# Attention in pieces of four heads, keys built by halves, and the output norm's mean subtracted from kept partial sums in DRAM by adding DMAs

## The chip, the cores and the metric

The kernel runs on one core of a Trainium2 chip. The metric is the device time of one execution in microseconds (us). Three runs before the change gave 1446.03, 1446.87 and 1447.19 us; the median is 1446.87. A profile is one more execution, taken with the hardware profiler.

Engines are named as in the profile: PE is TensorE (matrix products), with PEld for its weight loads, DVE is VectorE, ACT is ScalarE, POOL is GpSimd, SP is SyncE. DMAs are issued by SP (queue q1), by GpSimd (queue q0), and a few by ScalarE (q10). They all run on the core's 16 DMA engines. Only GpSimd's queue carries adding DMAs, which add the source to what the destination holds.

## The reference, cut to what matters

One layer over 1024 tokens and 2048 channels, all in float32:

```python
h = x @ w_in + b_in
q, k, v, g_attn, u_pool, g_pool = split(h)
a = banded_sink_attention(q, k, v, sinks, bias, valid) * silu(g_attn)
b = multiscale_pool(u_pool, w_pool, pool_scale) * silu(g_pool)
mix = concat([a, b]) @ w_out
ple = sigmoid(x @ w_gate_ple) * (p @ w_ple)
out = layer_norm(alpha * x + mix + ple, ln_gain, ln_bias)   # over the 2048 channels
```

Attention has 16 query heads of 64 and two key/value heads, each for eight query heads. A block of 128 queries sees its own and the previous block of keys; a learned sink joins each softmax. The norm first subtracts each token's mean over the channels.

## The kernel before, in words

**Layout and products.** Activations are kept as blocks of 128 channels by tokens, so the 2048 output channels are 16 blocks (`NB`), and the 1024 tokens come as two halves of `T` = 512. A float32 product is made from three fp32r products: each operand is split into a rounded high part and a low rest, and `mm3` (L182 to L185) issues high by high, low by high, high by low. ScalarE casts the high part (`wh`, L815), VectorE makes the low part (`wl`, L126). Large products use a Winograd scheme with seven products per pair of blocks (`p1` to `p7`); a pair is a `Job`, and the last two jobs of a stage, as the first two, run side by side.

**Stages.** `s1` and `s2` make keys, values and queries and the first half of everything else; `s3` finishes gates, pooling and the embedding; `s4` and `s5` are the two halves of the output product; `s6` is its rest. `s4` leaves 16 partial sums `co` in DRAM, 1024 tokens wide. `s5` adds the other half of the product for the first `F1` = 768 tokens in the Winograd scheme (384 columns to a matmul), `s6` does the last `F2` = 256 tokens plainly. In `s5` a job's result is finished by an adding DMA on GpSimd's queue, `part += co` (L436, `finished`); six steps later the result is squared for the norm (`norm_square`, L1022). The four blocks of the last two jobs go the other way: their `co` is loaded ahead into `filled` tiles, and products are added to it. In `s6` the rest of each `co` is loaded, and products are added.

**The mean.** The weights of the second half (`wc`) are centred in advance, so only the partial sums `co` carry a mean. While `s4` runs, `csum` adds up all 16 `co`; `mean_to_subtract` (early in `s5`) sums it over the 128 partitions by a product with ones and scales it by -1/2048 (L997). For blocks 4 to 7 `first_done` adds it on VectorE. For the other blocks `less_mean` (L1012) adds it by one more matmul per PSUM bank: operands `z` are the high and low part of the mean, stacked on 64 partitions each.

**Steps.** The program is written as a sequence of steps. One step is one product of a job (12 matmuls) and whatever is due then: `self.after(n, fn)` runs `fn` n steps on, `self.later(n, fn)` does so and holds its instructions behind the marked ones of that time. The tile framework then orders the instructions of each engine by this sequence among those that are ready, and sets the waits. Each engine runs its instructions in the order that results, and stops at one that has to wait. GpSimd's DMAs use eight semaphores in turn, so one waits until the eighth before it has landed.

**Units ahead.** A weight unit (a pair `wh`, `wl`) is made four products ahead (`take`), in a pool of four.

**Attention.** `heads(h, j)` handles two heads (block `j` of the queries) over one half `h` of the tokens: four query blocks `bq`. It runs beside `s2`, one call every nine steps. Scores (L607) are four matmuls of 256 keys, VectorE adds the bias and takes the maximum (L609), ScalarE takes exponentials (L623) and shares (L636), TensorE transposes (L643), and `value` (L663) multiplies by values (`vv`) and by the differences of neighbouring value blocks (`vd`), which take back what a window leaves out (`affine_select`, L651). Keys and values of the second key/value head are built after the eighth call: `k_build` for both halves in one go at step t+71, `v_build` by halves.

**The start.** `ple_inputs` loads the first embedding weights in two pieces with the first piece of `p` between; `ple_half` (L873) starts with products that need high parts only.

Of the kernel before, what the change touches and what calls it, by code (L numbers as in the profile page):

```python
# [31 lines left out]
P = 128  # L32
# [24 lines left out]
class Job:  # L57


    def __init__(self, w, b0, b1, half, first, done, tokens=2 * T, plain=False, ahead=None):  # L60
        self.ahead, self.filled, self.mean, self.apart, self.wait = ahead, False, False, False, 4
        self.w, self.b, self.half, self.first, self.done = w, (b0, b1), half, first, done
        self.tokens, self.plain = tokens, plain


class Layer:
# [396 lines left out]
    def product(self, job, o, s):  # L463
# [8 lines left out]
        mean = {"p1": 0, "p5": n}.get(o) if job.mean else None  # L472
        with self.in_turn("PE"):
            for k in range(4):
                f = slice(k * P, (k + 1) * P)
                mm = self.mm3(ps, (wh[:, f], wl[:, f]), (xh[:, k], xl[:, k]), k == 0 and o in s, k == 3 and mean is None)
# [22 lines left out]
    def run_plain(self, g):  # L499
# [3 lines left out]
        for i in range(2):  # L503
            ps = self.bank(BANKS[0][i], 2)[:, :F2]
            final = job.mean and i
            for u in range(2):
                wh, wl = self.take()
                for k in range(4):
                    f = slice(k * P, (k + 1) * P)
                    mm = self.mm3(ps, (wh[:, f], wl[:, f]), self.x_plain(4 * u + k), u + k == 0, False)  # L510
# [3 lines left out]
                if u:  # L514
                    mm = self.less_mean(ps, F1)
# [12 lines left out]
    def k_build(self, g, src):  # L528
# [5 lines left out]
        for h in range(2):  # L534
# [40 lines left out]
    def heads(self, h, j):  # L575
# [3 lines left out]
        rq, qs, sc, pt, old, pv, pre, bias = [], [], {}, {}, {}, {}, [], []  # L579

        def begin():
            rq.append(self.fetch(self.qd[j][:, h * T : h * T + T]))
            bias.append(self.slot()[:, :T].rearrange("p (e k) -> p e k", e=2))
            self.load(bias[0], self.rel[j])
# [10 lines left out]
        def k0(bq):  # L595
            return P if h == 0 and bq == 0 else 0

        def score(bq):
            sc[bq] = self.slot()[:, :T].rearrange("p (e k) -> p e k", e=2)
            ps = self.bank("sc", 2, (P, 2, 256))  # L600
            z = k0(bq)

            keys = slice((4 * h + bq - 1) * P + z, (4 * h + bq + 1) * P)
            for e in range(2):
                q = qs[e][:, bq * P : (bq + 1) * P]
                for i, kk in enumerate(self.kk):
                    nc.tensor.matmul(ps[:, e, z:], q, kk[:, keys], start=i == 0, stop=i == 1)  # L607
            for e in range(2):
                nc.vector.tensor_tensor_reduce(  # L609
                    out=sc[bq][:, e, z:], in0=ps[:, e, z:], in1=bias[0][:, e, z:], op0=ALU.add, op1=ALU.max, scale=1.0,  # L610
                    scalar=self.c(C_SINK + 8 * j + 2 * bq + e), accum_out=mx[:, 2 * bq + e : 2 * bq + e + 1])

        def shift(bq):
            f = slice(2 * bq, 2 * bq + 4)
            nc.vector.tensor_scalar(out=neg[:, f], in0=mx[:, f], scalar1=-1.0, scalar2=None, op0=ALU.mult)
            self.tt(sk[:, f], self.c(C_SINK + 8 * j + 2 * bq, 4), neg[:, f], ALU.add)
            nc.scalar.activation(sk[:, f], sk[:, f], AF.Exp)

        def softmax(bq):
            z, h2 = k0(bq), slice(2 * bq, 2 * bq + 2)  # L620
            for e in range(2):
                i = 2 * bq + e
                nc.scalar.activation(sc[bq][:, e, z:], sc[bq][:, e, z:], AF.Exp, bias=neg[:, i : i + 1],  # L623
                                     accum_out=den[:, i : i + 1])
            self.tt(den[:, h2], den[:, h2], sk[:, h2], ALU.add)
            nc.vector.reciprocal(out=rec[:, h2], in_=den[:, h2])

            cur = sc[bq][:, :, P:]
            if z == 0:
                self.tt(cur, sc[bq][:, :, 0:P], cur, ALU.add, nc.gpsimd)  # L630

        def share(bq):
            cur = sc[bq][:, :, P:]
            for e in range(2):
                i = 2 * bq + e
                nc.scalar.activation(cur[:, e], cur[:, e], AF.Copy, scale=rec[:, i : i + 1])  # L636

        def trans(bq):
            ps = self.bank("tr", 1)
            for i in range(2):  # L640
                for e in range(2):
                    o = (2 * i + e) * P
                    nc.tensor.transpose(ps[:, o : o + P], sc[bq + i][:, e, P:], self.ident)  # L643
            for i in range(2):
                t = ps[:, 2 * i * P : 2 * i * P + 2 * P].rearrange("p (e q) -> p e q", e=2)
                both = pt[bq + i] = self.slot(F32R)[:, :T].rearrange("p (s e q) -> p s e q", s=2, e=2)
                nc.scalar.copy(out=both[:, 0], in_=t)
                self.lo(both[:, 1], t, both[:, 0])
                if not k0(bq + i):
                    a = old[bq + i] = self.slot(F32R)[:, :T]  # L650
                    nc.gpsimd.affine_select(out=a.rearrange("p (c q) -> p c q", c=4), in_=both.rearrange("p s e q -> p (s e) q").bitcast(F32), pattern=[[0, 4], [-1, P]],  # L651
                                            compare_op=ALU.is_ge, fill=0.0, base=-1, channel_multiplier=1)

        def value(bq):
            if bq % 2 == 0:
                pv[0] = self.bank("pv", 1, (P, 2, 2, P))
            ps = pv[0]
            ms = [(self.vv[h][:, bq], pt[bq].rearrange("p s e q -> p (s e q)"))]
            if not k0(bq):
# [874 lines left out]
```

## Time and profile before

| | |
|---|---|
| median of three runs | 1446.87 us |
| the profiled execution, its span | 1447.21 us, 1445.5 us |
| first matmul of `s5`, of `s6`, and last of `s6` (start) | 1260.7, 1382.0, 1432.0 us |
| granted TensorE clock over the span | 0.997 |

A page gives busy time by engine, the span in 40 slices, the DMA queues, the chain of work that ended last and the costliest groups. Other views of the same trace group instructions by line and shape, list who waited for whom, show the instructions in order of time, and sum busy times or DMA traffic over a chosen stretch. Start times count from the start of the span. A matmul's duration overlaps that of the next one, so what a matmul takes of TensorE is the distance between two starts.

### The profile page before, as it was taken

The numbers are of one execution on the slowest core, as the hardware profiler recorded it, in microseconds if no ns is written. First come the engines' busy times: TensorE is split into PE (matmuls) and PEld (weight loads), VectorE is DVE, ScalarE is ACT, GpSimd is POOL, SyncE is SP. The second block draws the span as 40 slices with busy tenths as digits, with TensorE's granted clock in tenths as the row PEclk, the third lists the DMA queues.
The fourth block names the chain that finished last, engine by engine and source line by source line (L and its number), as shares of the span: only waits on it lengthen the run. The fifth ranks groups of instructions, "written<-read, shape, count | busy, mean of one in ns | idle before, by whom it ended". The sixth has DMA issues, their size and how long they took to land.

```text
span 1445.5 us, 20558 instructions
## 1 busy us (share of the span) xinstructions
PE 1429.9 (99%) x6940; PEld 1216.4 (84%) x6940; DVE 1118.4 (77%) x2078; ACT 795.8 (55%) x1598; POOL 233.4 (16%) x339
## 2 busy tenths in 40 slices
PE   9999999999999999999999999999999999999996
PEld 7888888888888888888888888888888888899996
DVE  6859578888788888888768876867678666987787
ACT  6646376665666666566664444442456433654476
POOL 0000202122122111112101211111001211111223
PEclk9999999999999999999999999999999999999998
DMA  9463886454455454556887879998699768594476
GB/s 357 181 241 119 228 221 193 164 178 161 146 183 211 166 178 162 183 208 205 225 248 208 229 205 285 338 277 269 197 297 314 210 184 229 136 280 113 114 236 234
DMA packets 112457, 307.67 MB, mean 213 GB/s; under 512 B 12832, under 2 KB 18592, under 8 KB 112352
## 3 DMA queue, kind: packets, MB, share of 16 engines
q1 hardware_dynamic: 87712, 225.88, 45.6%
q0 software_dynamic: 21312, 73.15, 21.4%
q10 hardware_dynamic: 3328, 7.34, 1.5%
q8 instruction: 54, 0.88, 0.3%
q14 instruction: 51, 0.42, 0.1%
HBM read 207.75 MB, written 98.57 MB: 212 GB/s over the span
## 4 chain that ended last, share of the span: by engine, by line
PE 95%; DVE 2%; DMA 1%; ACT 1%; issue 0%; POOL 0%; SPq 0%; POOLq 0%; DVEq 0%; ACTq 0%
PE qa L183 16%; PE qa L184 16%; PE qa L185 16%; PE qb L184 12%; PE qb L183 12%; PE qb L185 12%; PE sc L607 2%; PE pv L663 2%; PE sc L185 1%; PE sc L183 1%; PE sc L184 1%; PE tr L643 1%; DMA cw<-in_wout 1%; PE tr L873 1%; PE pv L873 1%
## 5 line engine op out<-in xcount | busy, mean ns | idle before, releaser
L815 ACT CAST wh<-raw 128x512 fp32r<-128x512 f32 x428 | 264.1, 619 | 371.6 <-PE qa L184 142.6
L126 DVE TENSOR_TENSOR wl<-raw,wh 128x512 fp32r<-128x512 f32 x428 | 297.1, 698 | 106.6 <-ACT wh L815 101.9
L423 ACT COPY part<-qa 128x512 f32<-128x512 f32 (+1 forms) x180 | 103.9, 577 | 81.8 <-PE qa L185 79.3
L126 DVE TENSOR_TENSOR part<-part,qb 128x512 f32<-128x512 f32 (+1 forms) x120 | 81.3, 677 | 45.5 <-PE qb L185 38.8
L183 PE MATMUL qa<-b11h,wh 128*128 128x512 f32 (+2 forms) x292 | 109.2, 374 | 0.4 <-ACT part L423 0.4
L183 PE MATMUL qb<-b21h,wh 128*128 128x512 f32 (+2 forms) x292 | 109.1, 374 | 0.0
L185 PE MATMUL qa<-b11h,wl 128*128 128x512 f32 (+2 forms) x292 | 108.9, 373 | 0.0
L184 PE MATMUL qa<-b11l,wh 128*128 128x512 f32 (+2 forms) x292 | 108.9, 373 | 0.0
L185 PE MATMUL qb<-b21h,wl 128*128 128x512 f32 (+2 forms) x292 | 108.8, 372 | 0.0
L184 PE MATMUL qb<-b21l,wh 128*128 128x512 f32 (+2 forms) x292 | 108.7, 372 | 0.0
L183 PE MATMUL qa<-t4h,wh 128*128 128x512 f32 (+1 forms) x260 | 100.0, 385 | 0.5 <-DVE part L126 0.5
L183 PE MATMUL qa<-t2h,wh 128*128 128x512 f32 (+1 forms) x260 | 100.3, 386 | 0.1
L183 PE MATMUL qb<-t1h,wh 128*128 128x512 f32 (+1 forms) x260 | 100.2, 385 | 0.0
L183 PE MATMUL qb<-b22h,wh 128*128 128x512 f32 (+1 forms) x260 | 100.1, 385 | 0.0
L183 PE MATMUL qa<-t3h,wh 128*128 128x512 f32 (+1 forms) x260 | 100.1, 385 | 0.0
L185 PE MATMUL qa<-t2h,wl 128*128 128x512 f32 (+1 forms) x260 | 99.9, 384 | 0.0
L185 PE MATMUL qb<-t1h,wl 128*128 128x512 f32 (+1 forms) x260 | 99.8, 384 | 0.0
L185 PE MATMUL qb<-b22h,wl 128*128 128x512 f32 (+1 forms) x260 | 99.8, 384 | 0.0
L185 PE MATMUL qa<-t3h,wl 128*128 128x512 f32 (+1 forms) x260 | 99.8, 384 | 0.0
L184 PE MATMUL qa<-t2l,wh 128*128 128x512 f32 (+1 forms) x260 | 99.8, 384 | 0.0
L184 PE MATMUL qb<-b22l,wh 128*128 128x512 f32 (+1 forms) x260 | 99.8, 384 | 0.0
L184 PE MATMUL qa<-t3l,wh 128*128 128x512 f32 (+1 forms) x260 | 99.8, 384 | 0.0
(336 smaller groups left out, 3537.8 us busy)
## 6 DMA issues: line engine op xcount, KB each, us to landing
raw<-in_win SPq DMA_DIRECT2D x65, 512.0 KB, 4.2
h<-part SPq DMA_DIRECT2D x34, 512.0 KB, 2.9
part<-h POOLq DMA_DIRECT2D x34, 512.0 KB, 6.6
cw<-in_wout SPq DMA_DIRECT2D x64, 256.0 KB, 3.1
raw<-in_wgate SPq DMA_DIRECT2D x32, 512.0 KB, 4.4
raw<-wc SPq DMA_DIRECT2D x32, 512.0 KB, 4.3
s<-in_x SPq DMA_DIRECT2D x44, 256.0 KB, 6.6
wc<-cw SPq DMA_DIRECT2D x32, 256.0 KB, 2.4
```

Of the source, the lines that this page charges most:

```text
L126: return (eng or self.nc.vector).tensor_tensor(out=out, in0=a, in1=b, op=op)
L183: mm(ps, wh, xh, start=start, stop=False, skip_group_check=True)
L184: mm(ps, wh, xl, start=False, stop=False, skip_group_check=True)
L185: return mm(ps, wl, xh, start=False, stop=stop, skip_group_check=True)
L423: self.mark("ACT", self.nc.scalar.copy(out=dst, in_=ps))
L607: nc.tensor.matmul(ps[:, e, z:], q, kk[:, keys], start=i == 0, stop=i == 1)
L643: nc.tensor.transpose(ps[:, o : o + P], sc[bq + i][:, e, P:], self.ident)
L663: nc.tensor.matmul(ps[:, bq % 2], w, t, start=i == 0, stop=i == len(ms) - 1)
L815: ins = self.nc.scalar.copy(out=out, in_=a)
L873: mm = self.nc.tensor.matmul(ps[b], w[u][:, b, k], p[v], start=k == 0 and u + v == 0, stop=k == 1 and at in ((3, 5) if n == 0 else (4, 5)) ...
```

## The change

Five things change.

- **The mean.** `less_mean` is no longer a matmul. When the total is scaled, 28 adding DMAs on GpSimd's queue add it to `co` in DRAM: 12 of 128x768 (all blocks but 4 to 7) and 16 of 128x256. The 12 + 16 matmuls and the preparation of `z` go. The loads of the `filled` blocks, which now have to follow, move from step 20 to 26 of `s5`, those of the last operand from 30 to 34.
- **Attention.** A call of `heads` handles two query blocks of four heads (`j` and `j + 1`) over half of a token half. Each `value` matmul has 512 columns instead of 256. Scores come two to a step. Queries, bias and results are moved by two DMAs each per call instead of one.
- **Keys** of the second head are built by halves, at steps t+65 and t+77.
- **The start.** The first embedding weights are loaded and split in one piece, and `ple_half` uses `mm3` block by block.
- Two steps that split the operands of `s4` move from 26 and 30 to 28 and 31.

```diff
@@ product / run_plain
-        mean = {"p1": 0, "p5": n}.get(o) if job.mean else None
...
-        if mean is not None:
-            mm = self.less_mean(ps, mean)
...
-                if u:
-                    mm = self.less_mean(ps, F1)
@@ k_build
-        for h in range(2):
+        for h in src:
@@ heads
-    def heads(self, h, j):
+    def heads(self, h, j, half):
...
+            for i in range(2):
+                self.load(two(q)[:, i], self.qd[j + i][:, f])
+            for i in range(2):
+                bias.append(self.slot()[:, :T].rearrange("p (e k) -> p e k", e=2))
+                self.load(bias[i], self.rel[j + i])
...
+        def value(n):
+            ps = self.bank("pv", 1)
+            ms = [(self.vv[h][:, block(n)], t) for t in pt[n]]
+            if not none(n):
+                ms += [(self.vd[h][:, block(n) - 1 + h], t) for t in old[n]]
             for i, (w, t) in enumerate(ms):
-                nc.tensor.matmul(ps[:, bq % 2], w, t, start=i == 0, stop=i == len(ms) - 1)
+                nc.tensor.matmul(ps, w, t, start=i == 0, stop=i == len(ms) - 1)
...
-        for bq in range(4):
-            t = 4 * (bq // 2)
-            self.after(5 + 2 * bq, lambda bq=bq: score(bq))
...
+        for n in range(2):
+            for i in range(2):
+                self.after(6 + 4 * n, lambda n=n, i=i: score(n, i))
+            self.after(9 + 4 * n, lambda n=n: shift(n))
+            self.after(15 + 4 * n, lambda n=n: trans(n))
...
+            self.after(21 + 4 * n, lambda n=n: value(n))
@@ ple_inputs / ple_half
-        self.load(first[:, 0, : T // 2], w[:, 0, : T // 2])
+        self.load(first[:, 0], w[:, 0])
...
-                for at, (b, u, v) in enumerate(((0, 0, 0), (0, 1, 0), (1, 0, 0), (0, 0, 1), (1, 0, 1), (1, 1, 0)) if n == 0 else
...
+                for b in range(2):
+                    mm = self.mm3(ps[b], tuple(t[:, b, k] for t in w), tuple(t[:, 2 * h + k] for t in self.ple_p), k == 0, k == 1)
@@ mean_to_subtract / less_mean
-        step = self.one["new"]("q")[:, :h]
...
-    def less_mean(self, ps, k):
-        return self.nc.tensor.matmul(ps, self.w64, self.z[k], start=False, stop=True, skip_group_check=True)
+    def less_mean(self, b, f):
+
+        self.nc.gpsimd.dma_start(out=self.co[b][:, f], in_=self.total[:, f], accum_op=ALU.add)
@@ run
-            self.after(t - 2 + 9 * i, lambda i=i: self.heads(i % 2, i // 2))
-        self.after(t + 63 + 8, lambda: build_kv(KB, self.k_build, 1))
+            self.after(t - 2 + 9 * i, lambda i=i: self.heads(i // 2 % 2, i // 4 * 2, i % 2))
+        for h, n in enumerate((65, 77)):
+            self.after(t + n, lambda h=h: build_kv(KB, self.k_build, 1, (h,)))
...
-                    self.after((10, 13, 16, 19, 22, 26, 30)[n], step)
+                    self.after((10, 13, 16, 19, 22, 28, 31)[n], step)
...
-            self.after(20 + 2 * b, lambda b=b: self.load(flat(filled[b]), co[b][:, :F1]))
+            self.after(26 + 2 * b, lambda b=b: self.load(flat(filled[b]), co[b][:, :F1]))
...
+        for n, b in enumerate((8, 9, 0, 1, 2, 3, *range(10, NB))):
+            self.after(12 + n, lambda b=b: self.less_mean(b, slice(0, F1)))
+        for b in range(NB):
+            self.after(24 + b, lambda b=b: self.less_mean(b, slice(F1, 2 * T)))
```

What this does to the order on three engines. First GpSimd, early in `s5`, before: `co_212` to `co_227` are the partial sums of blocks 0 to 15, `d` and `part` the results to which L436 adds them.

```order
L145 DMA co_227<-part_11883 128x1024
L436 DMA d_12243<-co_216 128x768
L436 DMA d_12245<-co_218 128x768
L436 DMA d_12244<-co_217 128x768
L436 DMA d_12246<-co_219 128x768
L436 DMA part_12557<-co_220 128x768
L436 DMA part_12558<-co_221 128x768
```

After the change, from the same place (L991 is the new `less_mean`, `csum` the scaled total):

```order
L145 DMA co_227<-part_11760 128x1024
L991 DMA co_220<-csum_11224 128x768
L991 DMA co_221<-csum_11224 128x768
L436 DMA d_12120<-co_216 128x768
L991 DMA co_212<-csum_11224 128x768
L436 DMA d_12122<-co_218 128x768
L991 DMA co_213<-csum_11224 128x768
L436 DMA d_12121<-co_217 128x768
L991 DMA co_214<-csum_11224 128x768
L436 DMA d_12123<-co_219 128x768
L991 DMA co_215<-csum_11224 128x768
L991 DMA co_222<-csum_11224 128x768
```

Five more large ones follow (`co_223` to `co_227`), then the first small ones, and only then the sums of blocks 8 and 9 (`co_220`, `co_221`):

```order
L991 DMA co_227<-csum_11224 128x768
L991 DMA co_212<-csum_11224 128x256
L991 DMA co_213<-csum_11224 128x256
L991 DMA co_214<-csum_11224 128x256
L991 DMA co_215<-csum_11224 128x256
L991 DMA co_216<-csum_11224 128x256
L991 DMA co_217<-csum_11224 128x256
L991 DMA co_218<-csum_11224 128x256
L436 DMA part_12423<-co_220 128x768
L436 DMA part_12424<-co_221 128x768
```

So the `d` sums stand behind two to five other DMAs that were not there, and the two `part` sums behind 19.

Second ScalarE, where the results of blocks 8 and 9 are squared, after the change (before, the same instructions stand here in the same order):

```order
L811 CAST wh_12661<-raw_12358 128x512
L423 COPY part_12581<-qb_12644 128x384
L1001 ACTIVATE q_12680<-part_12423 128x768
L1001 ACTIVATE q_12682<-part_12424 128x768
L811 CAST wh_12684<-raw_12358 128x512
L423 COPY part_12581<-qa_12586 128x384
```

TensorE uses that unit, `wh_12684`, in the second product of the job of blocks 12 and 13 (`qb`, operand `b21`), at this place:

```order
L184 MATMUL qa_12736<-b11l_11807,wh_12661 128x384
L185 MATMUL qa_12736<-b11h_11806,wl_12662 128x384
L183 MATMUL qb_12755<-b21h_11861,wh_12684 128x384
L184 MATMUL qb_12755<-b21l_11862,wh_12684 128x384
L185 MATMUL qb_12755<-b21h_11861,wl_12685 128x384
```

The matmul with the mean that stood between the two products is gone.

Third TensorE in the attention: the values of two query blocks of two heads before (x2 are two matmuls with one weight tile),

```order
L663 MATMUL pv_2526<-s_2351,v_436_1861 128x256 x2
L663 MATMUL pv_2526<-s_2354,d_437_1862 128x256 x2
L643 MATMUL tr_2531<-ident,s_2190 128x128 x2
L643 MATMUL tr_2531<-ident,s_2256 128x128 x2
L183 MATMUL qb_2550<-t1h_1339,wh_2447 128x512
```

and those of one query block of four heads after:

```order
L185 MATMUL qb_2546<-t1h_1336,wl_2443 128x512
L660 MATMUL pv_2565<-s_2344,v_437_1861 128x512
L660 MATMUL pv_2565<-s_2345,v_437_1861 128x512
L660 MATMUL pv_2565<-s_2348,d_438_1862 128x512
L660 MATMUL pv_2565<-s_2349,d_438_1862 128x512
```

Half as many value matmuls are left, each twice as wide.

More of the change, by code (lines that the diff above doesn't have):

```diff
@@ L609, in score @@
                 nc.vector.tensor_tensor_reduce(
[L610 to L614, printed above, removed]
+                    out=s[:, e, z:], in0=ps[:, e, z:], in1=bias[i][:, e, z:], op0=ALU.add, op1=ALU.max, scale=1.0,
+                    scalar=self.c(C_SINK + 8 * (j + i) + 2 * block(n) + e), accum_out=mx[:, c : c + 1])
```

162 lines of the change are left out of this document (67 added, 95 removed).

## The prediction

> **What bounds the kernel now.** I read the page's busy shares and the shares of its chain first, then a table of stretches over the last two stages, then the groups by shape, and last the DMA queues.
>
> ```profile
> span 1445.5 us, 20558 instructions
> PE 1429.9 (99%) x6940; PEld 1216.4 (84%) x6940; DVE 1118.4 (77%) x2078; ACT 795.8 (55%) x1598; POOL 233.4 (16%) x339
> PE 95%; DVE 2%; DMA 1%; ACT 1%; issue 0%; POOL 0%; SPq 0%; POOLq 0%; DVEq 0%; ACTq 0%
> ```
>
> TensorE (PE) is busy nearly throughout and is 95% of the chain that ends last. So there are two ways to move the time: TensorE gets less to do, or it waits more or less. The profiled execution took 1447.2 us, 1.7 around its span of 1445.5, and 0.3 over the median of 1446.87; the sum is made against 1447.2.
>
> ```profile
> 1340.00:1360.00 20.00, 20.00 (x117) 20.00 (x116) 14.34 (x25) 8.07 (x15) 1.74 (x2) 1.00 0.55 116
> 1405.00:1432.00 27.00, 27.00 (x230) 26.95 (x229) 25.60 (x46) 22.87 (x36) 11.18 (x21) 1.00 0.81 286
> 1432.00:1445.50 13.50, 2.01 (x16) 1.65 (x14) 5.52 (x11) 5.50 (x10) 4.60 (x8) 0.64 0.47 155
> ```
>
> The first is inside s5, the second inside s6 (columns: length, then PE, PEld, DVE, ACT, POOL busy, then clock, DMA share, GB/s). TensorE has no gap in either. The last 13.5 us are the second norm and its output, which the change leaves alone.
>
> **Matmuls that go.**
>
> ```profile
> L1012 PE MATMUL qb<-two,w 128*128 128x256 f32 x8 | 2.2, 281 | 0.0
> L1012 PE MATMUL qa<-two,w 128*128 128x256 f32 x8 | 2.2, 281 | 0.0
> L1012 PE MATMUL qb<-two,w 128*128 128x384 f32 x6 | 2.0, 340 | 0.0
> L1012 PE MATMUL qa<-two,w 128*128 128x384 f32 x6 | 2.0, 339 | 0.0
> 1323.98 0.34 PE L1012 MATMUL qa<-two,w 128*128 128x384 f32 x1
> 1324.16 0.34 PE L183 MATMUL qb<-b21h,wh 128*128 128x384 f32 x1
> 1425.75 0.28 PE L1012 MATMUL qb<-two,w 128*128 128x256 f32 x1
> 1425.87 0.28 PE L183 MATMUL qa<-b11h,wh 128*128 128x256 f32 x1
> ```
>
> The 0.34 us of one overlaps the next; what it costs is start to start, 0.18 us and 0.12 us. So 12 x 0.18 = 2.2 us go from s5 and 16 x 0.12 = 1.9 us from s6. In the stretch of 27 us about 9 of 230 matmuls go, 1.1 us, and VectorE has 1.4 us free there, so the gain stays.
>
> ```profile
> L663 PE MATMUL pv<-s,v 128*128 128x256 f32 x128 | 25.5, 280 | 0.0
> L663 PE MATMUL pv<-s,d 128*128 128x256 f32 x112 | 22.4, 282 | 0.0
> 244.26 0.47 PE pv L663 x4
> 9.10 2.72 PE qa L873 x12
> ```
>
> The values: 240 matmuls of 256 columns at 0.47/4 = 0.118 us become 120 of 512 at 2.72/12 = 0.227 (another line's, the same shape): 28.2 - 27.2 = 1.0 us less. Scores and transposes keep their number.
>
> ```profile
> PE sc L607 <- DVE s L126: 0.5, 2, 0.3
> PE sc L607 <- DVE st L609: 0.4, 1, 0.4
> PE tr L873 <- ACT t4h L849: 0.7, 1, 0.7
> ```
>
> All waits of TensorE for a score's operands lie at 633 to 655 us, where the second group's keys and values are built: 0.9 us. Keys by halves, and a score one step later after its queries' split, should end them: I take 0.9 (bounds 0 and 0.9).
>
> The start gets slower. There the second matmul of a product now needs the low part of p, where before three products of the high part came first:
>
> ```profile
> 7.40 0.69 DVE L126 TENSOR_TENSOR t4l<-two,t4h 128x512 fp32r<-128x512 f32 x1 [1.76 <-ACT t4h L849]
> ```
>
> This low part is ready at 8.1 us; five matmuls of 0.227 behind it end at 9.2, against 8.7 now, less what the second piece of p gains by being issued one DMA earlier (0 to 0.5): +0.3 (bounds 0 and 0.6). Sum so far: -2.2 - 1.9 - 1.0 - 0.9 + 0.3 = **-5.7 us**, 1441.5.
>
> **What the adding DMAs cost.** No adding DMA into DRAM is in this trace. The nearest are those from DRAM into SBUF, of the same 384 KB and 3 KB rows, on the same queue (q0); plain transfers bound them from below:
>
> ```profile
> d<-co POOLq DMA_DIRECT2D x2, 384.0 KB, 6.5
> q0 software_dynamic: 548, 1.52, 100.0%
> q1 hardware_dynamic: 305, 1.13, 99.7%
> part<-co POOLq DMA_DIRECT2D x6, 384.0 KB, 4.9
> ```
>
> The second row is the stretch 1290 to 1298, where only adding DMAs run on q0: all 16 engines are full with 1.52 MB in 8 us, so one of 0.393 MB holds them for 2.07 us. The third is 1281 to 1284, plain loads: 1.13 MB in 3 us, 1.04 us for the same size. An add reads two operands, so I take 2.07 (ends: 1.04, and half as much again, 3.1, should the write into DRAM cost a pass of its own), and a third of that, 0.69, for the 128 KB ones. One alone lands 4.9 us after its issue, so 2.8 us are issue and landing.
>
> Now the queue. The totals are ready when ScalarE's second scaling ends; the sums of blocks 8 and 9 are wanted by two squares:
>
> ```profile
> 1282.31 1.09 ACT L997 ACTIVATE csum<-sc 128x512 f32<-128x512 f32 x2
> 1306.69 1.75 POOL L436 DMA_DIRECT2D part<-co  x2 [12.09 <-DVE part L126]
> 1316.35 1.58 ACT L1022 ACTIVATE q<-part 128x768 f32<-128x768 f32 x2
> 1317.83 0.61 ACT L815 CAST wh<-raw 128x512 fp32r<-128x512 f32 x1
> ```
>
> Today GpSimd issues the two sums at 1306.69, they land in 5 to 7 us, and the squares at 1316.35 don't wait. In the changed order of GpSimd, 12 large and 7 small adding DMAs and the four d sums stand ahead of them, all ready from 1283.4 on. Work ahead of and with them on q0: 12 x 2.07 + 6 x 2.07 + 7 x 0.69 = 42.1 us; so they land no sooner than 1283.4 + 2.8 + 42.1 = 1328.3. Beside them run the transfers of SP's queue:
>
> ```profile
> q1 hardware_dynamic: 1878, 3.88, 28.5%
> 1296.77 2.66 SPq L140 DMA_DIRECT2D raw<-wc  x2
> ```
>
> These take 28.5% of the 42 us from 1284 to 1326, 12 us, and the four loads of filled blocks that move in here add 4 x 1.04. Of these 16 us I take half as delaying q0 (bounds 0 and 16): landing at **1336**. By the Trainium skill, DMA: Bandwidth & Descriptors, section Issuing engines are not separate DMA queues, transfers from all issuers interleave on the same 16 engines; by that all 16 us would count, and the result below would be 1464.
>
> Behind the squares on ScalarE stands the cast of a weight unit, the one for the product that starts at 1324.16 (its row is above): with four units at most in hand, TensorE starves there. After the landing come one square (0.8), the cast (0.6), VectorE's low part (0.7) and some 0.3 of handing over, 2.4 us: TensorE restarts at 1338.4, **14.2 us late**. VectorE meets the queue already at block 5's sum, seventh in it (1286.2 + 7 x 2.07 = 1300.7, its add runs at 1297.6 now); such an earlier wait is part of the 14.2, not on top, since the landing does not move. The next pair of sums stands behind nine small DMAs (6.2 us) and is wanted 15 us later: no second wait. SP's two raw loads at 1296.77 stand behind filled blocks 2 and 3 (1303 to 1315 now) and are first cast near 1324: hidden; if not, inside the same wait.
>
> By the Trainium skill, TensorE: Matmul & The Clock Gate, section Part 1, an idle of about 3.4 us halves the clock until as much time has been busy, some 1.7 us more per long wait. The clock of 0.64 in the last stretch above agrees; by that rule the sum would be about 1458.
>
> I cost the rest at nothing: the pooled splits, one and two steps later, stay two steps (2.7 us each, 12 x 0.227) ahead of their products; the added loads of queries and bias are prefetched six steps ahead. If that cover went, each is a wait of 1 to 2 us.
>
> **Sum:** 1447.2 - 5.7 + 14.2 = 1455.7, so 1456.
>
> **Rivals.** (1) *Faster.* An adding DMA into DRAM costs little more than a store. With a price p the landing is 1306.6 + 14.3 p; at 1.04 it is 1321.5, before TensorE starves: no wait, 1441.5. It decides at p = 1.46, where the wait eats the 5.7. For it: both operands are only streamed. Against it: every adding row here costs twice a plain one. The skill's page on DMA, section Anatomy of one DMA, fits bytes/436e3 to a software DMA, 0.9 us here, which would give this case; the 2.07 measured for adds disagrees. (2) *No change.* SP's transfers fit into gaps of q0: landing 1328.3, a wait of 6.5, 1448. Against it: q0 alone is at 100%. (3) *Much slower.* Price 3.1: landing 1351, a wait of 29, 1471. (4) *Attention waits.* Two scores fall into one step:
>
> ```profile
> L609 DVE CUSTOM_DVE_ANT_0 s<-sc,s,cst 128x256 f32<-128x256 f32 x112 | 50.5, 477 | 5.8 <-PE sc L607 5.4
> ```
>
> Four reductions, 1.9 us of a step of 2.7, can hold VectorE's weight parts back; at 0.2 us in each of 32 steps that is 6 us, without the DMA wait 1448 and with it 1462.
>
> **Chances.** Forecast 0.57 (own range 1450 to 1464), rival 1 0.23, rival 2 0.10, rival 3 0.07, rival 4 0.03. A measurement of this kernel can tell about 0.2%, 2.9 us, from no change. Faster 0.23, within 0.10, slower 0.67. The range of 1440.5 to 1467 takes in rivals 1, 2 and 4 and the upper bound of SP's share; rival 3 is left out.
>
> **What would show it.** Right: GpSimd's adding DMAs from about 1280 on, each longer in the queue; squares of blocks 8 and 9 waiting for a DMA for 15 us or more; TensorE idle in s5 for 10 us or more; s5 and s6 otherwise 4 us shorter. Wrong: no wait of ScalarE there, and adding DMAs that move 0.393 MB in less than 1.4 us. The values' line must show 120 matmuls, and no wait near 640.

## The result and the profile after

The changed kernel took 1478.01 us (median of four runs, 1477.71 to 1480.23) against 1446.45 us before (median of four, with one run of 1445.63 more than the three above): ratio 1.0217, 95% interval 1.0204 to 1.0230. It is slower by 31 us, where 9 were forecast. The profiled execution took 1478.2 us. Its page, in the lines that answer to those of before:

```profile
span 1476.5 us, 20365 instructions
PE 1432.4 (97%) x6792; PEld 1211.2 (82%) x6792; DVE 1112.2 (75%) x2041; ACT 789.3 (53%) x1559; POOL 257.2 (17%) x367
PE 84%; DMA 5%; DVE 4%; issue 3%; POOL 1%; ACT 1%; SPq 1%; POOLq 0%; DVEq 0%; ACTq 0%
```

TensorE has 148 matmuls less and yet is busy for longer. Its share of the chain fell from 95% to 84%; DMAs, VectorE and "issue" came in. A table of stretches tells where; here are s5 and s6 of before (columns as in the prediction: length, then PE, PEld, DVE, ACT, POOL busy, clock, DMA share, GB/s):

```profile
1260.70:1382.00 121.30, 121.12 (x690) 119.99 (x689) 97.12 (x152) 61.53 (x110) 22.22 (x33) 1.00 0.68 184
1382.00:1432.00 50.00, 50.00 (x426) 49.95 (x426) 45.35 (x80) 39.31 (x64) 16.96 (x29) 1.00 0.70 236
```

and of after:

```profile
1259.00:1413.90 154.90, 127.60 (x679) 124.26 (x678) 94.93 (x148) 59.00 (x104) 46.82 (x61) 0.90 0.81 187
1413.90:1462.30 48.40, 48.03 (x410) 47.50 (x409) 45.23 (x80) 38.85 (x64) 16.95 (x29) 1.00 0.68 239
```

Up to s5 the profiled execution gained 1.7 us (it starts at 1259.0, not 1260.7). s6 is 1.6 shorter. s5 is 33.6 longer, and that is more than the whole loss. It splits by the busy column: 27.3 us of TensorE idle (before: 0.2), and 127.6 us busy where 121.1 less twelve matmuls of 0.18, 119.0, was due, so 8.6 us of slowed matmuls; the mean granted clock is 0.90 (in the four us behind each of four restarts it is 0.50, 0.60, 0.57 and 0.57, which makes some 7 of the 8.6). Together 27.1 + 8.6 - 2.1 = 33.6.

What TensorE waited for, over the whole program of after (us in total, times, longest):

```profile
PE qb L183 <- ACT wh L811: 16.6, 2, 16.4
PE qa L183 <- ACT part L423: 4.5, 3, 2.2
PE qa L183 <- DVE part L126: 4.3, 1, 4.3
PE qa L183 <- ACT d L423: 3.4, 1, 3.4
PE qa L183 <- ACT wh L811: 0.7, 1, 0.7
```

The order of time of GpSimd shows the adding DMAs (L991; the sums are L436). The bracket is the idle time before an instruction and what ended it:

```profile
1282.21 1.80 POOL L991 DMA_DIRECT2D co<-csum  x2 [11.06 <-ACT csum L986]
...
1321.18 0.86 POOL L991 DMA_DIRECT2D co<-csum  x1 [2.18 <-issue]
...
1336.47 1.78 POOL L436 DMA_DIRECT2D part<-co  x2 [0.47 <-issue]
...
1353.46 0.88 POOL L436 DMA_DIRECT2D part<-co  x1 [0.77 <-DVE part L126]
```

GpSimd issues twelve large ones and four sums up to 1321.2, then seven small ones up to 1336; only then do the sums of blocks 8 and 9 go out, 30 us later than before (1306.69). The last row is the sum of block 10. ScalarE waits in front of the squares, and behind the second of them stands a weight cast:

```profile
1342.54 0.84 ACT L1001 ACTIVATE q<-part 128x768 f32<-128x768 f32 x1 [20.74 <-DMA part<-co]
1344.39 0.84 ACT L1001 ACTIVATE q<-part 128x768 f32<-128x768 f32 x1 [1.00 <-DMA part<-co]
1345.13 0.60 ACT L811 CAST wh<-raw 128x512 fp32r<-128x512 f32 x1
...
1361.87 0.85 ACT L1001 ACTIVATE q<-part 128x768 f32<-128x768 f32 x1 [3.12 <-DMA part<-co]
```

And TensorE, which the list of waits ties to a weight cast, is really tied to these sums: the cast stands behind the squares. Its order of time around the long wait:

```profile
1329.08 0.34 PE L185 MATMUL qa<-b11h,wl 128*128 128x384 f32 x1
1345.79 0.69 PE L183 MATMUL qb<-b21h,wh 128*128 128x384 f32 x1 [16.37 <-ACT wh L811]
...
1349.31 0.34 PE L185 MATMUL qb<-b21h,wl 128*128 128x384 f32 x1
1351.90 0.45 PE L183 MATMUL qa<-t2h,wh 128*128 128x384 f32 x1 [2.24 <-ACT part L423]
...
1352.60 0.52 PE L183 MATMUL qa<-t2h,wh 128*128 128x384 f32 x1
1352.92 0.52 PE L184 MATMUL qa<-t2l,wh 128*128 128x384 f32 x1
```

This is the product that the prediction placed at 1324.16 before and 1338.4 after; it starts at 1345.79. For 3 us behind the wait a matmul takes 0.52 us, and the next starts 0.32 later, not 0.18.

### The profile page after: what moved, and what is told of

The parts are those of the page before. It is cut to its first block, busy times and chain, and to the rows that moved or that the text cites. A ratio compares the mean times of both kernels' runs of the same rounds, so it can differ in the third digit from the quotient of the medians.

```text
span 1476.5 us, 20365 instructions
## 1 busy us (share of the span) xinstructions
PE 1432.4 (97%) x6792; PEld 1211.2 (82%) x6792; DVE 1112.2 (75%) x2041; ACT 789.3 (53%) x1559; POOL 257.2 (17%) x367
## 4 chain that ended last, share of the span: by engine, by line
PE 84%; DMA 5%; DVE 4%; issue 3%; POOL 1%; ACT 1%; SPq 1%; POOLq 0%; DVEq 0%; ACTq 0%
PE qa L183 14%; PE qa L185 14%; PE qa L184 14%; PE qb L185 11%; PE qb L183 11%; PE qb L184 11%; PE sc L608 2%; PE pv L660 2%; PE sc L185 1%; PE sc L183 1%; PE sc L184 1%; DVE wl L126 1%; DMA part<-co 1%; DMA cw<-in_wout 1%; DMA wc<-cw 1%
## 5 line engine op out<-in xcount | busy, mean ns | idle before, releaser
L423 ACT COPY part<-qa 128x512 f32<-128x512 f32 (+1 forms) x180 | 103.9, 577 | 74.8 <-PE qa L185 74.2
L183 PE MATMUL qb<-b21h,wh 128*128 128x512 f32 (+2 forms) x292 | 109.7, 376 | 16.6 <-ACT wh L811 16.6
L183 PE MATMUL qa<-b11h,wh 128*128 128x512 f32 (+2 forms) x292 | 109.0, 373 | 0.6 <-ACT part L423 0.6
L183 PE MATMUL qa<-t2h,wh 128*128 128x512 f32 (+1 forms) x260 | 101.4, 390 | 6.3 <-ACT d L423 3.4
L183 PE MATMUL qa<-t4h,wh 128*128 128x512 f32 (+1 forms) x260 | 100.6, 387 | 4.3 <-DVE part L126 4.3
L183 PE MATMUL qa<-t3h,wh 128*128 128x512 f32 (+1 forms) x260 | 99.9, 384 | 1.7 <-ACT part L423 1.7
L185 PE MATMUL qa<-t4h,wl 128*128 128x512 f32 (+1 forms) x260 | 100.4, 386 | 0.0
L184 PE MATMUL qa<-t4l,wh 128*128 128x512 f32 (+1 forms) x260 | 100.3, 386 | 0.0
L183 PE MATMUL qb<-t1h,wh 128*128 128x512 f32 (+1 forms) x260 | 100.2, 385 | 0.0
L183 PE MATMUL qb<-b22h,wh 128*128 128x512 f32 (+1 forms) x260 | 99.8, 384 | 0.0
```

What stands on the lines that cost most here:

```text
L183: mm(ps, wh, xh, start=start, stop=False, skip_group_check=True)
L184: mm(ps, wh, xl, start=False, stop=False, skip_group_check=True)
L185: return mm(ps, wl, xh, start=False, stop=stop, skip_group_check=True)
L423: self.mark("ACT", self.nc.scalar.copy(out=dst, in_=ps))
```

## The experiments

Theory Q throughout: the loss is the queue, that is, adding DMAs that stand ahead of sums that are wanted soon. The runs first ask which part of the change costs, then what in the queue.

**The change with the mean back on TensorE** (the diff's parts on the mean undone, all others kept):

```diff
+        for j in s5[2:]:
+            j.mean = True
...
-            self.after(12 + n, lambda b=b: self.less_mean(b, slice(0, F1)))
```

> The changed kernel with the mean subtracted by matmuls again, as before the change; attention, keys, start and pooled splits stay changed. Theory Q (the whole loss is block sums that stand behind the adding DMAs on GpSimd's queue): 1444 to 1446 us, since the part of the program ahead of s5 is 1.6 us shorter in the changed kernel's trace and s5 goes back to 121 us. Rival H (attention or another part of the change costs as well): above 1450.

Measured: 1448.38 us (before in the same series 1447.07), ratio 1.0002, interval 0.9992 to 1.0011. The 30 us are gone with the adding DMAs. But the gain that was expected of attention, keys and start isn't there either; the expectation missed by 2.4 us. One row of its list of waits shows a part of why:

```profile
PE qa L183 <- ACT part L423: 3.7, 3, 1.3
```

Before, this was 0.4 us, one time, at 1108 us. Here the three lie at 235.8, 487.3 and 1109.0 us (1.3, 1.0 and 1.3); scores and values run from 198 to 685 us, so the first two, 2.3 us, are products beside attention that wait for ScalarE, and the third is not. Of the 0.9 us of waits for scores that the prediction wanted to end, 0.7 stays (`PE sc L613 <- DVE st L616: 0.7, 1, 0.7`). In this trace s5 starts at 1261.45, 0.75 us later than before, though 120 value matmuls are gone. In the changed kernel's trace the same waits are one beside attention of 1.7 and one of 0.6 in s4, so their size differs from one trace to the other, and no run takes the three parts one by one.

**The kernel before with only the adding DMAs** (the other way about: the diff's parts on the mean alone):

```diff
-        for j in s5[2:]:
-            j.mean = True
...
+        for n, b in enumerate((8, 9, 0, 1, 2, 3, *range(10, NB))):
+            self.after(12 + n, lambda b=b: self.less_mean(b, slice(0, F1)))
+        for b in range(NB):
+            self.after(24 + b, lambda b=b: self.less_mean(b, slice(F1, 2 * T)))
```

> The kernel before with only the adding DMAs in place of the mean's matmuls (and the loads that move with them). Theory Q: 1478 to 1481 us, s5 155 us long. Rival H: 1446 to 1455.

Measured: 1476.73 us, one run; 1447.07 before. That is 1.3 under theory Q's range, with an s5 of 151.7 us and not 155, and far above rival H's. Theory Q holds: the mean's DMAs alone make the loss.

**Plain stores in place of adding ones:**

```diff
-        self.nc.gpsimd.dma_start(out=self.co[b][:, f], in_=self.total[:, f], accum_op=ALU.add)
+        self.nc.gpsimd.dma_start(out=self.co[b][:, f], in_=self.total[:, f])
```

> The changed kernel with the 28 DMAs as plain stores of the total over the partial sums, in the same order with the same waits; the addition is left out, so the output is not the norm's. Theory Q with time in the queue set by the double reading of an add: a large one holds the engines 1.0 instead of 2.0 us, the sums of blocks 8 and 9 land 12 to 17 us earlier (1326 to 1331 instead of 1343), TensorE waits 0 to 5 us there: 1443 to 1453 us. Rival W (the number of DMAs on GpSimd and their waits count, not what each moves): above 1468.

Measured: 1452.68 us, one run. With the same 28 DMAs at the same place, 25 of the 31 us go, and the square of block 8 starts at 1324.05, 18.5 us earlier; so it is mainly the adding DMA's time on the queue, and not the number of DMAs or the waits that they add. Waits of TensorE of 2.2, 1.6 and 2.0 us stay in s5; the 5.6 us that are left are not taken apart further.

**The same 28 adding DMAs behind the block sums** (four large ones behind the sums of 7, 9 and 11 each, the small ones behind 13 and 15):

```diff
-            self.after(12 + n, lambda b=b: self.less_mean(b, slice(0, F1)))
...
+        self.behind_sum[of[7]] = [(b, big) for b in (8, 9, 0, 1)]
+        self.behind_sum[of[9]] = [(b, big) for b in (2, 3, 10, 11)]
...
+        self.behind_sum[of[15]] = [(b, small) for b in range(10, NB)]
```

> The changed kernel with the same 28 adding DMAs, each held on GpSimd's queue until it stands behind a block sum: blocks 8, 9, 0, 1 behind the sum of block 7, then 2, 3, 10, 11 behind that of 9, 12 to 15 behind 11, the small ones behind 13 and 15. Theory Q (order in the queue): no wait of 2 us or more of TensorE in s5, s5 and s6 about 3.5 us shorter than before: 1441 to 1444 us. Rival B (the traffic itself is too much for the 16 engines, in any order): above 1455, with waits spread over s5.

Measured: 1452.41 us, ratio 1.0038, interval 1.0023 to 1.0053. The order gives back 26 of 31 us, but not all; the time lies between the two theories' numbers. What stays are two waits of the same kind, smaller and for later blocks: 3.2 us behind the squares of blocks 10 and 11, and 2.4 us late in s5. Two pieces of the chain of the first, in order of time:

```profile
1319.49 9.79 DMA co<-csum x2
1329.90 8.40 DMA part<-co
```

The adds into blocks 10 and 11 were the last two of their group of four; the sum of the same block had to wait for them, and then took 8.4 us itself.

**The 12 large ones alone** (the kernel before, with the large adding DMAs at the change's place and the small means by matmuls):

```diff
-        for j in s5[2:]:
-            j.mean = True
...
+        for n, b in enumerate((8, 9, 0, 1, 2, 3, *range(10, NB))):
+            self.after(12 + n, lambda b=b: self.add_mean(b, slice(0, F1)))
```

> The kernel before with only the 12 large adding DMAs, at the place where the change has them; the 16 small ones aren't there, and their mean is subtracted by matmuls of s6 as before. To be compared with the run that had all 28 on the kernel before (1476.7, with waits of TensorE in s5 of 4.2, 0.7 and 16.1 us up to the landing of the sums of blocks 8 and 9, then 2.2 and 3.5 us, and 5.6 us of matmuls at half clock). Seven small ones stood ahead of the sums of blocks 8 and 9: 7 x 0.69 = 4.8 us less there; s6 gets 1.9 us longer. Theory V (the later waits come from VectorE, whose last addition to blocks 10 and 11 stood behind blocked work): they stay, 1476.7 - 4.8 + 1.9 = 1473.8, between 1471 and 1475. Theory S (the later waits come from the nine small DMAs between the two pairs of sums): they vanish, and about half of the half-clock loss with them: 1473.8 - 5.7 - 2.9 = 1465, between 1462 and 1468.

Measured: 1464.24 us, one run: theory S by the number. The small ones, a third of the bytes that are added, make 12.5 us of the loss when they stand behind the large ones. With all 28 on the kernel before, the first square of block 8 starts at

```profile
1343.04 0.84 ACT L1006 ACTIVATE q<-part 128x768 f32<-128x768 f32 x1 [19.81 <-DMA part<-co]
```

and with the large ones alone at

```profile
1333.76 0.84 ACT L1026 ACTIVATE q<-part 128x768 f32<-128x768 f32 x1 [9.32 <-DMA part<-co]
```

GpSimd began 0.2 us earlier here (1283.95, not 1284.17), so seven small adding DMAs delayed the landing by 9.1 us, 1.3 each; the prediction took 0.69. TensorE's three longest waits in s5 with the large ones alone:

```profile
PE qa L184 <- DVE part L127: 5.4, 1, 5.4
PE qb L184 <- ACT wh L816: 5.1, 1, 5.1
PE qa L184 <- ACT part L424: 2.3, 1, 2.3
```

Of the two later waits that the run with all 28 had, the one of 3.5 us is gone (in the changed kernel it is the row `PE qa L183 <- ACT d L423`), and one of 2.3 us behind the restart stays. Theory S is right for the first; the second stays, as theory V has it.

**Small ones alone, two behind each sum from block 6 on; the same with large ones two by two; the same with large means on VectorE:**

```diff
+        order = [*range(4, NB), *range(4)]
+        for n in range(8):
+            self.behind_sum.setdefault(of[6 + n], []).extend((b, slice(F1, 2 * T)) for b in order[2 * n : 2 * n + 2])
...
+        for n, p in ((7, (8, 9)), (9, (10, 11)), (11, (12, 13)), (13, (14, 15))):
+            self.behind_sum[of[n]] = [(b, slice(0, F1)) for b in p]
...
-            if 4 <= b < 8:
+            if 4 <= b:
```

The first piece is in all three, the second in the run with the large ones, the third in the one with VectorE.

> The kernel before, with the mean of the first 768 columns subtracted by matmuls as before, and only the 16 small partial sums (128 KB each) corrected by adding DMAs, two of them directly behind each of the sums of blocks 6 to 13 on GpSimd's queue. Theory Q (the loss of the change is only the place of its adding DMAs ahead of sums that are wanted soon): the 16 x 0.69 = 11 us of transfer fall into the half idle DMA engines of s5 and nothing waits; 16 matmuls of 0.12 us go from s6: 1447.1 - 1.9 = 1445.2, between 1444.0 and 1446.5. Rival E (adding DMAs into DRAM disturb the other transfers wherever they stand, by their time on the 16 engines): some of the 11 us comes back as waits of TensorE in s5, 1449 or more.

> The kernel before with 24 adding DMAs: the large ones of blocks 8 to 15 two by two, each pair one pair of block sums ahead of the sums that need it (behind the sums of 7, 9, 11 and 13), and the 16 small ones as in the run of small ones alone; the four filled blocks keep their matmuls. Theory Q: 8 x 2.07 + 11 = 27.6 us of transfer fit into s5, where about 36 us of the DMA engines were idle, and the sums land before they are wanted: 8 x 0.18 + 16 x 0.12 = 3.4 us less, 1443.7, between 1442.5 and 1445.5. Rival E: the fuller DMA engines make one of the sums or a weight load late, a wait of over 3.4 us and some half-clock matmuls behind it: 1447 to 1453.

> The kernel before with the large means of blocks 8 to 15 subtracted on VectorE (as blocks 4 to 7 have it: 0.96 us each) in place of 8 matmuls, the small ones by the 16 adding DMAs placed as in the run of small ones alone, the filled blocks by their matmuls. Theory Q: VectorE has about 9 us of 40 free in s5, a block's 1.9 us of every 15 fit, and no large adding DMA is there: 3.4 us less, 1443.7, between 1442.5 and 1445.5. Rival F (VectorE becomes what the weights wait for): 0.3 us or more in each of the six steps, with the sums 1.9 us late for the squares: 1446 or more.

Measured, with 1447.69 us before: small ones alone 1447.92, ratio 0.9998 (0.9987 to 1.0008); with large ones 1456.44, ratio 1.0061 (1.0049 to 1.0074); with VectorE 1447.43, ratio 0.9999 (0.9990 to 1.0008). All three miss theory Q's numbers. In the first, s6 is 1.8 us shorter and s5 gives it back. Its stretches:

```profile
1300.00:1310.00 10.00, 10.00 (x60) 10.00 (x59) 8.74 (x13) 5.06 (x9) 2.83 (x4) 1.00 0.69 160
1310.00:1312.00 2.00, 0.49 (x3) 0.18 (x2) 1.93 (x4) 0.65 (x2) 0.74 (x1) 1.00 1.02 177
1312.00:1316.00 4.00, 3.98 (x14) 3.43 (x15) 2.92 (x6) 1.53 (x3) 2.65 (x3) 0.70 0.81 122
```

TensorE idles for 1.5 us at 1310, and in the 4 us behind it runs at a clock of 0.70: 14 matmuls, where 23 would fit at the pace of the first row and 16 at that clock. The chain behind this wait starts at other sums than the expectation of the next run says, since block 9's was issued at 1312.81, after the wait:

```profile
1295.40 1.77 POOL L437 DMA_DIRECT2D d<-co  x2 [1.00 <-issue]
1300.08 0.96 DVE L127 TENSOR_TENSOR d<-d,csum 128x768 f32<-128x768 f32 x1 [2.48 <-DMA d<-co]
```

These are the sums of blocks 5 and 7. Two small DMAs stand ahead of them, and they went out at 1295.40 where before they did at 1289.97 and 1293.73. VectorE waited 2.48 us for one of them, and what it prepares for ScalarE's weight casts came late. So even adding DMAs that stand behind a sum cost, if another sum follows close. The run with VectorE has a wait of 1.8 us at the same place. The run with large ones lost 9 us, more than rival E gave it; its waits are 1.9 us at that place again, 1.7 and 3.4. It has the small ones between the sums too, so it doesn't tell which of the two kinds made the later ones.

**Small ones behind the second sum of a pair only** (four each behind 9, 11, 13 and 15), alone and with the large means of blocks 8 to 15 on VectorE:

```diff
-        for n in range(8):
-            self.behind_sum.setdefault(of[6 + n], []).extend((b, slice(F1, 2 * T)) for b in order[2 * n : 2 * n + 2])
+        for n in range(4):
+            self.behind_sum[of[9 + 2 * n]] = [(b, slice(F1, 2 * T)) for b in order[4 * n : 4 * n + 4]]
```

> The kernel before with only the 16 small adding DMAs, four of them behind each of the sums of blocks 9, 11, 13 and 15, so that none stands between two sums of a pair. With two behind each sum from block 6 on (1447.9, no change) the sum of block 9 was issued at 1312.8, 4.75 us behind that of block 8, TensorE waited 1.7 us at 1310 and 15 matmuls ran at half clock, 2.0 us: together more than the 1.8 us that s6 got shorter. Theory Q (the place within the pair made that): no wait and no half clock in s5, 1447.1 - 1.8 = 1445.3, between 1444.3 and 1446.5. Rival E (the adding DMAs cost by their 13 us on the 16 engines, wherever they stand): a wait of 1 us or more and half-clock matmuls in s5 again, 1447 or more.

> As the run of small ones late, and besides the large means of blocks 8 to 15 on VectorE in place of 8 matmuls. The run with small ones in between and these means on VectorE had s5 at 122.6 us with 1.9 us of waiting and 0.8 us at half clock; without those two 119.9, which is 1.4 less than before. Theory Q: 1445.3 - 1.4 = 1443.9, between 1442.8 and 1445.2. Rival F (VectorE's 7.7 us more make the weights or the sums late): 1445.5 or more, with a wait of TensorE for VectorE in s5.

Measured, with 1446.73 us before: 1446.04, ratio 0.9995 (0.9986 to 1.0004), and 1445.64, ratio 0.9990 (0.9979 to 1.0001). In the first, TensorE waits nowhere in s5; the two stages read

```profile
1260.70:1381.90 121.20, 121.02 (x690) 119.89 (x689) 96.70 (x151) 60.89 (x108) 36.42 (x49) 1.00 0.83 200
1381.90:1430.40 48.50, 48.00 (x412) 47.39 (x411) 45.29 (x80) 38.96 (x64) 16.96 (x29) 1.00 0.69 241
```

against 121.3 and 50.0 before: in the profile theory Q's 1.6 us are there, and rival E is wrong for this place. The second lies 0.4 us above theory Q's range; its trace has no wait of TensorE for VectorE in s5, as rival F wanted one. But the runs don't tell either kernel from the one before, so neither is shown to beat it. The same small DMAs that cost 12.5 us in the change cost nothing that the runs can show here (1.3 us is what they can tell). Two things differ from there: their place, and the twelve large ones, which are missing here. No run has one without the other.

This pair of profiles also gives the price by itself. GpSimd's queue between 1300 and 1380 us, before:

```profile
q0 software_dynamic: 1917, 5.24, 31.7%
```

and with the 16 small ones:

```profile
q0 software_dynamic: 4202, 7.31, 51.2%
```

19.5% of 80 us for 16 of them: 0.98 us of all 16 engines each.

**The loads of the filled blocks twelve steps later** (on the run of the large ones alone):

```diff
-            self.after(26 + 2 * b, lambda b=b: self.load(flat(filled[b]), co[b][:, :F1]))
+            self.after(38 + 2 * b, lambda b=b: self.load(flat(filled[b]), co[b][:, :F1]))
```

> The run of the 12 large adding DMAs alone (1464.2; waits of TensorE in s5 of 12.3 us up to the landing of the sums of blocks 8 and 9, then 2.5, and 4.4 us of matmuls at half clock), with one thing changed: SP loads the four filled blocks twelve steps later. These are 4 x 384 KB of the 5.43 MB that SP's queue moves in the 48 us from 1284 to 1332, where it has 33.3% of the 16 engines, 16.0 us; so they are 4.6 us. Theory W (SP's transfers delay GpSimd's queue by their whole time, where the prediction counted half): the sums land 4.6 us earlier, 1464.2 - 4.6 - 1 us of half clock = 1458.6, between 1456.5 and 1460.5. Rival G (they fit into gaps of GpSimd's queue, and its own price is higher than predicted): 1462.5 to 1465. Rival O (SP's raw weights behind the waiting loads are what TensorE lacks): more than 6 us less, under 1456.5.

Measured: 1463.26 us, one run; 1464.24 with the loads at their place. Theory W misses; the time is in rival G's range. The two queues from 1284 to 1332 us, with the large ones alone:

```profile
q0 software_dynamic: 2404, 6.60, 71.5%
q1 hardware_dynamic: 2445, 5.43, 33.3%
```

and with the loads later:

```profile
q0 software_dynamic: 2498, 6.85, 76.5%
q1 hardware_dynamic: 1921, 4.08, 26.8%
```

In both the two queues' shares add up to over 100% of the engines' time. SP's queue took 3.1 us less (a raw weight load more came in where the four had been), and the square of block 8 started at 1332.89, 0.9 us earlier, though GpSimd began 0.5 later (1284.42): 0.9 to 1.4 of 3.1 us. So SP's transfers delay GpSimd's queue by less than their time here, near the half that the prediction took. One run with one set of loads doesn't settle the share in general; that stays open.

**The large ones behind the sum of block 7** (again on the run of the large ones alone):

```diff
-            self.after(12 + n, lambda b=b: self.add_mean(b, slice(0, F1)))
...
+        self.behind_sum[of[7]] = [(b, slice(0, F1)) for b in (8, 9, 0, 1, 2, 3, *range(10, NB))]
```

> The run of the 12 large adding DMAs alone (1464.2), with all of them held behind the sum of block 7 on GpSimd's queue: the sums of blocks 4 to 7 are no longer among them, those of blocks 8 and 9 still stand behind all twelve. There TensorE waited 5.6 us at 1303.6 (VectorE's add to block 5 waits for its sum), 1.4 at 1317 and 5.3 at 1331.7 (the squares of blocks 8 and 9 wait). Theory P (the landing of the sums of 8 and 9 sets the end, and the earlier wait is part of that delay, as the prediction put it): the wait at 1303 vanishes and the one at 1332 grows to about 12, with fewer matmuls at half clock (one long wait in place of three, 1 to 2 us less): 1461 to 1465. Theory T (the earlier wait stands on top, or itself delays the sums): 1464.2 - 5.6 - 1.4 = 1457.2, between 1455.5 and 1459.5.

Measured: 1466.68 us, one run, beside 1449.08 before on that chip: 17.6 above before, where the run with the early wait is 16.6 above its own. The time lies 1.7 above theory P's range and 7 above theory T's; the waits are theory P's. Its two longest in s5:

```profile
PE qb L184 <- ACT wh L819: 14.4, 1, 14.4
PE qa L184 <- ACT part L424: 1.8, 1, 1.8
```

The 5.4 us for VectorE are gone, and the wait for the squares has grown from 5.1 to 14.4. The square of block 8 starts at 1337.56, 3.8 us later, though the large ones began 14 us later (1298.21). Which sum waits first changes little, 1.0 us: the landing of blocks 8 and 9 sets the end.

## Why the prediction was right in kind and wrong in size

The mechanism was the forecast one: sums of blocks 8 and 9 behind 12 large and 7 small adding DMAs, squares that wait, a cast behind them, TensorE starved. The size was 22 us off. By the prediction's steps:

- **Matmuls that go: right.** -2.2 and -1.9 were forecast. s6 is 1.6 shorter; the 120 value matmuls are there:

```profile
L660 PE MATMUL pv<-s,v 128*128 128x512 f32 x64 | 20.0, 393 | 0.0
L660 PE MATMUL pv<-s,d 128*128 128x512 f32 x56 | 17.3, 390 | 0.0
```

- **Values, keys and start, -1.6 together: not confirmed.** The profiled execution has it, but ten runs of the kernel with everything but the adding DMAs don't differ from before. In their trace new waits for ScalarE's copies (2.3 us beside attention, 0.9 more than before in s4) and a wait of 0.7 for a score, which the keys by halves should have ended, stand against it.
- **"I take 2.07": right.** In the changed kernel, from 1305 to 1328 us:

```profile
q0 software_dynamic: 1169, 3.15, 71.1%
```

71.1% of 23 us for 3.15 MB is 2.04 us for 0.393 MB. An add into DRAM costs here what one into SBUF cost before (2.07).
- **"A third of that, 0.69, for the 128 KB ones": wrong, and the dearest of the terms inside the landing.** They take 0.98 of the engines and delayed the queue by 1.3 each: 4.3 of the 7.0 us by which the landing was missed (1343.0 with the adding DMAs alone on the kernel before, whose start times the forecast of 1336 uses; 1342.5 in the changed kernel, whose s5 starts 1.7 us earlier). Bytes were scaled, but a 128 KB add in rows of 1 KB is dearer per byte than a 384 KB one in rows of 3 KB. From 1326 to 1336, when the changed kernel's small ones run nearly alone,

```profile
q0 software_dynamic: 931, 1.06, 78.6%
q1 hardware_dynamic: 60, 0.18, 5.0%
```

1.06 MB hold the engines for 7.9 us, 0.97 for each 0.131 MB. By the packets of the two rows of q0, one of 1.1 KB here holds an engine for 0.135 us and one of 2.7 KB there for 0.224: a third of the bytes isn't a third of the time. That fits a price by row; row length and size of the whole DMA weren't varied apart. A sixth of the engines' time is used by neither queue: they stand empty from 1330.5 to 1331.7, and GpSimd, idle from 1328.5 to 1330.3 with the mark issue, had sent out nothing since 1327.6. So part of the 1.3 us is GpSimd's pace and not the engines'; what held it there the trace doesn't show.

- **"Of these 16 us I take half": not the step that failed.** What is left of the landing's error, 2.7 us, has a start 0.8 us later in it (1284.17, not 1283.4). The Trainium skill, DMA: Bandwidth & Descriptors, section Issuing engines are not separate DMA queues, says that transfers of all issuers interleave; the two queues' shares with the large ones alone, 71.5% and 33.3%, or 104.8%, agree, but that all of SP's time counts the runs don't show.
- **The earlier wait "is part of the 14.2": right,** by the last run. TensorE idled 21.3 us up to its restart (16.4 + 4.3 + 0.7), 7.1 more than forecast.
- **"No second wait": wrong, 6.0 us.** Behind the restart TensorE idled for 27.3 - 21.3 us more. 3.4 of it goes when the small DMAs go, which stood between the two pairs of sums: nine of them were counted as 6.2 us, and with 1.3 each they are 12 of the 15 us that lie between. Another 2.2 us, a wait for ScalarE's copy of a result, followed the long wait in each run quoted above (1.8 to 2.3 us): the copy stands behind casts of weights that VectorE prepares, and VectorE had itself stood still for 22.1 us up to 1345.77.
- **The slow clock was left out of the sum: 8.6 us.** The prediction named it beside the sum, at 1.7 us per long wait, and left it out of it. There was not one wait but four (4.3, 16.4, 2.2 and 3.4 us), and the stretches behind them show it in the column of the clock, the third from the right:

```profile
1306.80:1328.60 21.80, 21.14 (x105) 20.28 (x106) 12.65 (x19) 6.73 (x12) 6.53 (x8) 0.89 1.07 270
1346.00:1352.00 6.00, 3.76 (x13) 3.21 (x13) 5.96 (x10) 2.31 (x6) 4.19 (x6) 0.75 0.87 96
1352.00:1368.50 16.50, 16.12 (x81) 15.48 (x82) 6.01 (x11) 4.94 (x9) 2.44 (x3) 0.90 0.65 134
1368.50:1378.00 9.50, 6.12 (x27) 5.81 (x26) 6.95 (x11) 3.55 (x7) 1.78 (x2) 0.82 0.70 135
```

So 22.5 us, the difference of the spans less the forecast 8.5, are 7.1 of longer waiting before the restart, 6.0 behind it, 8.6 of slow clock and 0.8 of the rest. The range failed because its upper end took in SP's share alone: the small DMAs' price had no bounds, and what follows a wait was in no term. Rival 3 comes nearest in time (1471), but by a price of 3.1 us for a large add, which was measured at 2.04; that nearness is luck.

## What to carry to other kernels

Before work is moved onto a queue that is served in order, look for what already stands there and is waited for soon, and price each kind of DMA from a transfer of its own size and row length, not by bytes. When a wait of TensorE is forecast, add what follows it: slow matmuls behind the restart, and the next waits, which the same queue makes. The same 16 small DMAs cost 12 us ahead of sums and behind twelve large ones, and nothing that could be measured alone and behind the second sum of a pair, so the place is better written into the program than left to the step at which the data happens to be ready.

## What was not expected of the hardware

The Trainium skill, TensorE: Matmul & The Clock Gate, Part 1, gives half clock after an idle window of about 3.4 us. The long wait agrees, and so do the other eight waits of 3.7 us or more in s5 of these runs: the clock of the first 2 us behind each is 0.50. But in the rows above 2.24 us of idle at 1349.7 were enough for matmuls at 0.52 us from 1352.6 on, 0.32 from start to start, 3.9 us after the last restart; and 1.5 us of idle at 1310 in the run of the small ones alone, after 10 us without a gap, lowered the clock to 0.70 over 4 us, 1.2 us lost. So a wait shorter than the rule's window can cost nearly as much again in clock. It doesn't always. With the adding DMAs alone on the kernel before, 3.35 us of idle end at 1372.91, and behind them TensorE runs at full pace:

```profile
1372.91:1376.91 4.00, 4.00 (x23) 4.00 (x24) 2.86 (x5) 1.47 (x3) 0.00 (x0) 1.00 0.93 173
```

In the changed kernel the same wait, 3.38 us, was followed by 14 matmuls in 4 us at a clock of 0.57. The three waits of 1.0 to 1.35 us with the mean back on TensorE left the clock at 1.00 too. Under 3.4 us the loss of clock is thus not a fixed price of a wait, and part of the 8.6 us above, 1.7 us behind this one wait, could as well have been absent. What decides between the two these traces don't show.
